# Zero writes to another queue, another order of experts and a rebuilt ending in a one-core transformer layer

## The chip, the cores and the metric

The program runs on 1 core of one Trainium2 chip. The metric is the device time of one execution in microseconds (us). The engines of the core are PE (TensorE; PEld is its weight load), DVE (VectorE), ACT (ScalarE), POOL (GpSimd) and SP (SyncE, which here only issues transfers). Transfers are issued by SP, ACT and POOL, each into a queue of its own, and are carried out by the core's 16 DMA engines.

## The reference, cut to what matters

One layer over 512 latent tokens of width 1024 and 256 context tokens: a modulated norm, one input projection, two branches (neighbourhood attention, and a gated DeltaNet that scans chunks of 64 tokens in two directions), an output projection, and then a mixture of 32 experts of which each token takes 4. The last part is

```
logits = xf @ w_router + b_router;  top_val, top_idx = top_k(logits, 4);  gates = softmax(top_val)
per expert:  g, u = split(x @ w1[e] + b1[e]);  h = min(g,7) * sigmoid(1.702*min(g,7)) * (clip(u,-7,7) + 1)
             y = h @ w2[e] + b2[e]
x = x1 + g2 * sum over the 4 experts of gate * y;   out = rmsnorm(x) * final_norm_w
```

w1 is (32, 1024, 2048), w2 (32, 1024, 1024), float32: 384 tiles of 1 MiB, all of which are read. Everything is computed to float32 accuracy; where a matmul uses the faster fp32r form, both operands are split into a high and a low part and three products are summed.

## The kernel before, in words

**Mixer** (`mixer`). Inputs and the first part of `w_mod` are loaded on SP (lines 923 to 949; `w_mod` in 16 loads of 512 KB through 4 buffers), the tokens are normalized, transposed and split, and then the input projection runs in pieces, whose weights ACT's queue loads (line 1005) and ACT and DVE split (lines 29, 30). `conv(2560, True)` makes the DeltaNet's v: six token tiles, each evicted by ACT (line 1391) and stored by ACT's queue to `vd` (line 1392). The planner that orders the instructions puts one on its engine as soon as its operands are there by the planner's own estimate; program order is its priority.

**Zeros.** `y4d` is a DRAM table of 2048 rows (token, choice), into which the experts scatter. It is cleared by nine stores from a small zero tile, eight of 1020 KB in pieces of 480 bytes and one small (lines 1338 to 1340). They stand before the DeltaNet's preparation in the program, on SP; they depend on nothing but the zero tile.

**Experts** (`moe`). Experts are ordered by load on the chip. A "large" one takes 128 token slots, a "small" one 64, and 16 are of each kind; expert 0 is large and fixed, then (before) odd ones are large and even ones small, and the last, 31, is small too. `Stream` loads the weight tiles in the order in which they are used, (e: gate half g), (e-1: w2), (e: up half u), four tiles each, through 10 buffers; `pump` issues the next load on SP when the tile ten places earlier is done. A small expert packs two half-width products into one bank, so that they run side by side. A large one runs g and u in plain float32 when e < 5, and in split fp32r from 5 on (`split_`); w2 is plain float32 always. From e = 2 on the order on PE, ACT and DVE is that of the program (`strict`). `fetch` gathers an expert's token rows from DRAM, `scatter` writes its weighted result to `y4d` (both on POOL's queue), except for experts 30 and 31, whose results are placed by one-hot matmuls (`last`).

**Second biases** (`second_bias`). At e = NE-2 = 30 the rows of b2 are loaded (SP), scaled by POOL, split by ACT and DVE; the gates are turned into a 96-row matrix by DVE and four transposes on PE.

**Ending** (lines 744 to 808). After the last expert's transposes the eight `y4d` tiles are taken, added on POOL and DVE to `x1` (lines 745 to 751); then comes a branch on the number of overflow blocks (`overflow`, line 596), and only after it the PE products into the output banks (`second`, `last`, `rest`), the last w2, the squares on ACT, and per token tile a reciprocal root on DVE in single-column instructions, two scalings by DVE (line 775) and the store (line 776). The weight tiles of the last w2 stand behind the `y4d` tiles in the stream:

```
self.order[-4:-4] = [(t, "y", c) for t in range(4) for c in range(2)]
```

Of the kernel before, what the change touches and what calls it, by code (L numbers as in the profile page):

```python
# [38 lines left out]
class Stream:  # L39
# [52 lines left out]

def small(e):

    return e == 31 or e > 0 and e % 2 == 0


def column(e):

    return e if e in (0, 31) else 15 + e // 2 if e % 2 == 0 else (e + 1) // 2  # L100
# [38 lines left out]
def moe(tc, ctx, cst, release, rps, rt, rtp, h2, hx, h2d, x1d, y4d, modd, w1, b1, w2, b2, fn_d, out, NE=32):  # L139
# [30 lines left out]
    PE, ACT, DVE = Engine(nc.tensor), Engine(nc.scalar), Engine(nc.vector)  # L170
# [61 lines left out]
    def split_(e):  # L232

        return not small(e) and e >= 5
# [78 lines left out]
    for i in range(4):  # L313
        nc.sync.dma_start(br[32 * i:32 * i + 32], dap(b1, 512 * (i // 2), [[2048, 32], [1024, 2], [1, 512]]))
# [94 lines left out]
    def second_bias(get, bs, Gt):  # L409

        br = get([96, 1024], F32, 0)
# [3 lines left out]
        nc.scalar.activation(bs, br, AF.Copy)  # L415
        nc.vector.tensor_tensor(bs[32:64], br[32:64], bs[32:64].bitcast(F32), op=OP.subtract)
        tmp = get([128, 16, 32], F32, 1)
        nc.vector.tensor_tensor(tmp, E, gt[:, :, None].to_broadcast([128, 16, 32]), op=OP.mult)
        G = get([128, 4, 3, 32], F32, 1)
        for i in range(3):  # L420
            nc.vector.tensor_reduce(G[:, :, i, :], tmp.rearrange("p (t k) e -> p t e k", k=4), axis=AX.X, op=OP.add)
        p = bank("tr")
        for t in range(4):
            nc.tensor.transpose(p[0:96, 128 * t:128 * t + 128], G[:, t].rearrange("p a e -> p (a e)"), ident)
        nc.scalar.activation(Gt, p[0:96, :], AF.Copy)
        nc.vector.tensor_tensor(Gt[64:96], p[64:96, :], Gt[64:96].bitcast(F32), op=OP.subtract)
# [82 lines left out]
    def mm(x, e, kind, after=None):  # L509
# [4 lines left out]
        p = [bank(tag) for _ in range(1 if s else 2)]  # L514
# [79 lines left out]
    def overflow(n, ovi, rowd, gatd):  # L594

        with tc.If(n > 0):
            with tc.For_i(0, n) as j:
                e = nc.values_load(ovi[0:1, bass.ds(j, 1)], min_val=0, max_val=31)
                with ExitStack() as s2:
                    lp = s2.enter_context(tc.tile_pool(name="ov_l", bufs=1))  # L600
                    pp_ = s2.enter_context(tc.tile_pool(name="ov_p", bufs=1, space=PSUM))
# [15 lines left out]
                    def tr(src, name):  # L617
                        T = lp.tile([128, 8, 128], F32, name=name)
                        for q in range(2):
                            p = pp_.tile([128, 4, 128], F32, name="tr", bufs=2)  # L620
                            for k in range(4):
                                nc.tensor.transpose(p[:, k, :], src[:, (4 * q + k) * 128:(4 * q + k + 1) * 128], ident)
                            nc.vector.tensor_copy(T[:, 4 * q:4 * q + 4], p)
                        return T

                    def lin(T, w, c0, b=None):
                        ps_ = [pp_.tile([128, 512], F32, name="mm%d" % i, bufs=2) for i in range(2)]
# [34 lines left out]
                    for t in range(4):  # L662
                        nc.vector.tensor_scalar(ot[:, t], iot, tf[:, t:t + 1], None, op0=OP.is_equal)
                        for i in range(2):
                            p = pp_.tile([128, 512], F32, name="mm%d" % i, bufs=2)
# [6 lines left out]
    def second(t):  # L672
        for n in range(2):
            LP[t, n] = bank(("h", "h", "tr", "y")[t])
            PE.matmul(LP[t, n], Gt[:, 128 * t:128 * t + 128], bs[:, 512 * n:512 * n + 512], start=True, stop=False)

    def last(t, i):

        for n in range(2):
            h = slice(64 * n, 64 * n + 64)  # L680
            PE.matmul(LP[t, n], ohT[i][h, t, :], yl[i][h, :], start=False, stop=i == 1)

    def rest(t):
        for n in range(2):
            PE.matmul(LP[t, n], ident, x1[:, t, 512 * n:512 * n + 512], start=False, stop=False)

    for e in range(NE + 1):
# [9 lines left out]
        if e == 4:  # L697
            wlo = hx.tile([128, 4, 1024], F32R, name="B")
        if e < NE:
# [6 lines left out]
            ahead(e, "u")  # L706
        if e == 2:
            strict[0] = False
            ovt = overflow_table()
            strict[0] = True  # L710
        if e == 3:
            strict[0] = False
            ovt = ovt()
            strict[0] = True
        if e == NE - 2:

            x1 = hx.tile([128, 4, 1024], F32, name="A")
            nc.sync.dma_start(x1, x1d.rearrange("(t p) d -> p t d", p=128))
# [4 lines left out]
            second_bias(areas([xp.tile([128, 1024], F32, name="yy", bufs=2) for _ in range(2)]), bs, Gt)  # L723
            for i in range(2):
                for t in range(1, 4):
                    nc.vector.tensor_scalar(tlast[:, i, t:t + 1], tlast[:, i, 0:1], -128.0 * t, None, op0=OP.add)
                for t in range(4):
                    nc.vector.tensor_scalar(ohT[i][:, t, :], iot, tlast[:, i, t:t + 1], None, op0=OP.is_equal)
        if e == NE:
            break  # L730
        if e:
            p = mm(TA.pop(e - 1), e - 1, "w2")
            if e < NE - 1:
                scatter(e - 1, weighted(e - 1, p, xp.tile([128, 1024], F32, name="yy", bufs=2)))
            else:
                weighted(e - 1, p, yl[0])
        nxt = e + 2 if 1 <= e < NE - 2 else None
# [7 lines left out]
    strict[0] = False  # L745
    for t in range(4):
        r = [stream.take(t, "y", c) for c in range(2)]
        nc.gpsimd.tensor_tensor(r[1][:, 0], r[1][:, 0], r[1][:, 1], op=OP.add)
        for q in (r[0][:, 0], r[0][:, 1], r[1][:, 0]):
            nc.vector.tensor_tensor(x1[:, t], x1[:, t], q, op=OP.add)  # L750
        stream.pump()
    xctx.close()
    pctx.close()
    overflow(*ovt)
    ps = pctx.enter_context(tc.tile_pool(name="moe_q", bufs=2, space=PSUM))

# [5 lines left out]
    strict[0] = True  # L762

    def squares(t):
        for n in range(2):
            ACT.activation(junk[:, 512 * n:512 * n + 512], LP[t, n], AF.Square, accum_out=sq[:, n, t:t + 1])

    def final(t):
        v = slice(t, t + 1)
        DVE.tensor_tensor(ss[:, 0, v], sq[:, 0, v], sq[:, 1, v], op=OP.add)  # L770
        DVE.tensor_scalar(ss[:, 1, v], ss[:, 0, v], 1.0 / 1024, 1e-6, op0=OP.mult, op1=OP.add)
        rsqrt1(nc, ss[:, 2, v], ss[:, 1, v], ss[:, 0, v])
        for n in range(2):
            c = slice(512 * n, 512 * n + 512)
            nc.vector.scalar_tensor_tensor(xf[:, t, c], LP[t, n], ss[:, 2, v], fnb[:, c], op0=OP.mult, op1=OP.mult)  # L775
        nc.sync.dma_start(out.rearrange("o (t p) d -> (o t) p d", p=128)[t], xf[:, t])

    for t in range(3):
        second(t)
        last(t, 0)  # L780

    def early(c):
        if c == 2:
            for t in range(3):
                rest(t)

    p = mm(TA.pop(NE - 1), NE - 1, "w2", early)
    weighted(NE - 1, p, yl[1])
    for t in range(3):
        last(t, 1)  # L790
        squares(t)
    second(3)
    rest(3)
    for i in range(2):
        last(3, i)
    squares(3)
    for t in range(4):
        final(t)
    pctx.close()
    wctx.close()  # L800
# [61 lines left out]
def rsqrt1(nc, r, v, t):  # L862

    nc.vector.tensor_scalar(r.bitcast(I32), v.bitcast(I32), -0.5, float(0x5F3759DF), op0=OP.mult, op1=OP.add)  # L864
    for c in (-3.0, -12.0, -768.0):
        nc.vector.scalar_tensor_tensor(t, r, v, r, op0=OP.mult, op1=OP.mult)  # L866
        nc.vector.scalar_tensor_tensor(r, t, c, r, op0=OP.add, op1=OP.mult)  # L867


def mixer(tc, ctx0, ctx, ctx2, cst, I, rope_d, mask_d, modd, x1d, h2d, y4d, rt, dbg=None, upto=99):  # L870
# [466 lines left out]

    for i in range(8):
        nc.sync.dma_start(dap(y4d, i * 2040, [[16384, 128], [120, 17], [1, 120]]), cst["zero"][:, None, :].to_broadcast([128, 17, 120]))
    nc.sync.dma_start(dap(y4d, 16320, [[16384, 128], [1, 64]]), cst["zero"][:, 0:64])  # L1340
# [582 lines left out]
```

## Time and profile before

| | us |
|---|---|
| runs, median of 3 (lowest to highest) | 1887.46 (1884.3 to 1888.91) |
| the profiled execution, its own time | 1889.57 |
| its span in the profile | 1887.5 |

Busy shares of the span on the page: PE 90%, DVE 50%, ACT 31%, POOL 14%; the DMA queues of SP, ACT and POOL hold 72.2%, 10.4% and 2.2% of the 16 engines' span. A busy PE is not a PE at its peak. Where the rows below are stretches, the columns are named with the first group.

### The profile page before, as it was taken

How to read it: one execution, taken by the hardware profiler on the slowest of the kernel's cores; microseconds unless marked ns; L12 is line 12 of the kernel's file. 1: busy time of each engine (PE TensorE's matmuls, PEld its weight loads, DVE VectorE, ACT ScalarE, POOL GpSimd, SP SyncE). 2: the span in 40 equal slices, each digit the busy share in tenths (PEclk: the TensorE clock that was granted, in tenths of full speed). 3: DMA queues.
4: the chain of work that ended last, by engine and by line, in shares of the span. 5: the costliest groups of instructions: out<-in, count | busy, mean ns of one | idle time of the engine just before them, and what ended most of it. 6: DMA issues, size and time to landing. Idle time of an engine off the chain costs nothing. (4 is left out here: it accounts for less than half of the span.)

```text
span 1887.5 us, 25145 instructions
## 1 busy us (share of the span) xinstructions
PE 1702.2 (90%) x9411; PEld 1031.8 (55%) x9411; DVE 952.7 (50%) x1555; ACT 590.6 (31%) x829; POOL 261.7 (14%) x251
## 2 busy tenths in 40 slices
PE   1798799999989988899999999999999999999666
PEld 0275587787767767444455545455545555455312
DVE  1246697883557676711254345444533553354243
ACT  1334347333235542100043224322422342243001
POOL 0030300323200241300010011011101110100020
PEclk7898999999999999899999999999999999999887
DMA  9845838756587653989999999999999999999991
GB/s 283 280 128 174 247 108 236 203 134 163 148 213 195 198 157 134 389 302 378 388 405 409 409 409 409 408 407 406 401 400 402 407 399 398 408 405 399 359 404 77
DMA packets 281122, 574.67 MB, mean 304 GB/s; under 512 B 79150, under 2 KB 142082, under 8 KB 280868
## 3 DMA queue, kind: packets, MB, share of 16 engines
q1 hardware_dynamic: 204248, 499.65, 72.2%
q10 hardware_dynamic: 69885, 57.00, 10.4%
q0 software_dynamic: 6864, 16.38, 2.2%
q8 instruction: 75, 1.23, 0.3%
q14 instruction: 50, 0.41, 0.1%
HBM read 529.68 MB, written 51.02 MB: 308 GB/s over the span
## 5 line engine op out<-in xcount | busy, mean ns | idle before, releaser
L165 PE MATMUL y<-raw,at 128*128 128x512 f32 (+1 forms) x1024 | 336.9, 595 | 0.0
L165 DVE TENSOR_TENSOR B<-raw,whi 128x2048 fp32r<-128x2048 f32 x104 | 236.6, 2289 | 162.3 <-ACT whi L165 162.2
L165 ACT ACTIVATE whi<-raw 128x2048 fp32r<-128x2048 f32 x104 | 198.6, 1915 | 119.1 <-DMA raw<-in_w_dram 92.0
L165 PEld LDWEIGHTS y<-raw,at 128*128 128x128 f32 (+1 forms) x1024 | 132.8, 164 | 186.0 <-issue 185.3
L165 PE MATMUL h<-raw,xts 128*64 128x512 f32 x1024 | 233.3, 598 | 0.0
L165 DVE TENSOR_SCALAR h<-h 128x512 f32<-128x512 f32 x96 | 65.0, 695 | 221.9 <-PE h L165 221.9
L1022 PE MATMUL pj<-hh,whi 128*128 128x512 f32 (+3 forms) x432 | 164.7, 384 | 6.8 <-ACT zb L1207 2.8
L1023 PE MATMUL pj<-hl,whi 128*128 128x512 f32 (+3 forms) x432 | 161.3, 376 | 0.0
L581 POOL DMA_INDIRECT y4d<-yy,rows x30 | 48.4, 1613 | 805.0 <-DVE yy L165 805.0
L1025 PE MATMUL pj<-hh,wlo 128*128 128x512 f32 (+3 forms) x432 | 159.1, 377 | 0.0
L165 PEld LDWEIGHTS h<-raw,xts 128*64 128x64 f32 x1024 | 68.1, 136 | 133.4 <-issue 132.8
L29 ACT ACTIVATE whi<-raw 128x512 fp32r<-128x512 f32 (+1 forms) x105 | 65.0, 626 | 188.9 <-PE pj L1023 78.2
L165 PE MATMUL h<-whi,xth 128*128 128x512 f32 x416 | 118.1, 406 | 6.4 <-ACT whi L165 6.2
L165 PE MATMUL h<-B,xth 128*128 128x512 f32 x416 | 116.1, 401 | 7.2 <-DVE B L165 7.2
L30 DVE TENSOR_TENSOR wlo<-raw,whi 128x512 fp32r<-128x512 f32 (+1 forms) x105 | 81.5, 781 | 70.1 <-ACT whi L29 68.5
L165 DVE SCALAR_TENSOR_TENSOR yy<-y,gates,g2b 128x512 f32<-128x512 f32 x32 | 24.0, 750 | 180.9 <-PE y L165 179.1
L165 PE MATMUL h<-whi,xtl 128*128 128x512 f32 x416 | 113.8, 395 | 0.0
L165 ACT ACTIVATE at<-tr 128x512 f32<-128x512 f32 x48 | 27.0, 596 | 258.2 <-PE tr L165 241.9
L1022 PEld LDWEIGHTS pj<-hh,whi 128*128 128x128 f32 (+1 forms) x432 | 82.4, 191 | 30.8 <-issue 4.6
L165 PEld LDWEIGHTS h<-B,xth 128*128 128x128 f32 x416 | 75.8, 188 | 35.9 <-DVE B L165 19.8
L165 PEld LDWEIGHTS h<-whi,xth 128*128 128x128 f32 x416 | 74.7, 188 | 34.1 <-ACT whi L165 17.7
L1023 PEld LDWEIGHTS pj<-hl,whi 128*128 128x128 f32 (+1 forms) x432 | 82.5, 191 | 14.8 <-issue 1.5
(485 smaller groups left out, 2460.1 us busy)
## 6 DMA issues: line engine op xcount, KB each, us to landing
raw<-in_w_dram SPq DMA_DIRECT2D x384, 1024.0 KB
raw<-in_w_in_dram ACTq DMA_DIRECT2D x44, 512.0 KB
raw<-in_w_mod_dram ACTq DMA_DIRECT2D x32, 512.0 KB
raw<-in_w_mod_dram SPq DMA_DIRECT2D x16, 512.0 KB
raw<-y4d SPq DMA_DIRECT2D x8, 1024.0 KB
y4d<-zero SPq DMA_DIRECT2D x8, 1020.0 KB
kk<-nkd SPq DMA_DIRECT2D x16, 384.0 KB
gad<-st ACTq DMA_DIRECT2D x16, 256.0 KB
```

The source lines that it names most:

```text
L29: nc.scalar.activation(hi, src, AF.Copy)
L30: nc.vector.tensor_tensor(lo, src, hi.bitcast(F32), op=OP.subtract)
L165: i = f(*a, **k)
L581: s = nc.gpsimd.indirect_dma_start(out=dst, out_offset=bass.IndirectOffsetOnAxis(ap=rows[:, k:k + 1], axis=0), in_=y, in_offset=None, boun ...
L1022: nc.tensor.matmul(p, h, mh(k), start=k == 0, stop=False)
L1023: nc.tensor.matmul(p, h, ml(k), start=False, stop=False)
L1025: nc.tensor.matmul(p, l, mh(k), start=False, stop=k == kb - 1)
```

## The change

It has these parts:

- **Zeros**: the nine stores go from SP to ACT's queue, two behind each store of v in four of the six token tiles (`issue_behind` fixes only the order of issue on that queue).
- **Order of experts**: 1 and 2 are small, then 15 large and 12 small ones are spread evenly over 3 to 29, 30 and 31 are small. Large ones are split from e = 3 on. The overflow table is made at e = 1 and closed at e = 2 (before 2 and 3).
- **First biases** b1 (four loads of 128 KB) go from SP's queue to POOL's.
- **Second biases**: b2 and `x1` are loaded by ACT's queue; the gate part runs behind expert 29's scatter, the transposed part behind expert 30's w2, all in program order.
- **Ending**: the `y4d` tiles of token tiles 0, 1 are loaded ahead of the last u, those of 2, 3 ahead of the last w2, and added there (`rows_of`); seven of the eight output banks get `second` and `last(., 0)` ahead of the last w2 and `rest` inside it; the reciprocal roots of token tiles 1 to 3 are taken together; two half tiles are scaled by ACT and POOL instead of DVE; the branch for overflow blocks comes behind the stores, and writes the output again if it is taken.

```
-        self.order[-4:-4] = [(t, "y", c) for t in range(4) for c in range(2)]
+        for i, t in ((-4, 2), (-12, 0)):
+            self.order[i:i] = [(t + c // 2, "y", c % 2) for c in range(4)]
+SMALL = [False, True, True] + [(12 * i + 25) // 27 > (12 * i + 13) // 27 for i in range(27)] + [True, True]
-        return not small(e) and e >= 5
+        return not small(e) and e >= 3
-        nc.sync.dma_start(br[32 * i:32 * i + 32], dap(b1, ...))
+        nc.gpsimd.dma_start(br[32 * i:32 * i + 32], dap(b1, ...))
-            nc.sync.dma_start(br[32 * i:32 * i + 32, :], b2.rearrange("o e f -> (o e) f"))
+            nc.scalar.dma_start(br[32 * i:32 * i + 32, :], b2.rearrange("o e f -> (o e) f"))
...
+    def rows_of(t):
+        r = [stream.take(t, "y", c) for c in range(2)]
+        POOL.tensor_tensor(r[1][:, 0], r[1][:, 0], r[1][:, 1], op=OP.add)
+        for q in (r[0][:, 0], r[0][:, 1], r[1][:, 0]):
+            DVE.tensor_tensor(x1[:, t], x1[:, t], q, op=OP.add)
+        stream.pump()
...
             else:
                 weighted(e - 1, p, yl[0])
+                turned_()
+                for t in range(2):
+                    rows_of(t)
...
     transp(NE - 1)
+    for t in range(2, 4):
+        rows_of(t)
+    p = [bank("y")]
+    seven = [(t, n) for t in range(4) for n in range(2)][:7]
+    for q in seven:
+        second(*q)
+        last(*q, 0)
+    def early(c):
+        if c == 2:
+            for q in seven:
+                rest(*q)
+    p = mm(TA.pop(NE - 1), NE - 1, "w2", early, p)
+    weighted(NE - 1, p, yl[1])
-    overflow(*ovt)
...
+    for q in seven:
+        last(*q, 1)
+    second(3, 1)
+    last(3, 1, 0)
+    rest(3, 1)
+    last(3, 1, 1)
+    for t in range(4):
+        squares(t, [LP[t, n] for n in range(2)])
+    factor(slice(0, 1))
+    for n in range(2):
+        scaled(0, n, LP[0, n])
+    store(0)
+    factor(slice(1, 4))
+    for t in (1, 2):
+        scaled(t, 1, LP[t, 1], True)
+    for t in (1, 2, 3):
+        scaled(t, 0, LP[t, 0])
+    for t in (1, 2):
+        store(t)
+    scaled(3, 1, LP[3, 1])
+    store(3)
...  copies of the eight banks to x1
+    overflow(*ovt)
+    with tc.If(ovt[0] > 0):
...
-    for i in range(8):
-        nc.sync.dma_start(dap(y4d, i * 2040, [[16384, 128], [120, 17], [1, 120]]), cst["zero"]...)
-    nc.sync.dma_start(dap(y4d, 16320, [[16384, 128], [1, 64]]), cst["zero"][:, 0:64])
...
-        nc.scalar.dma_start(vd[128 * t:128 * t + 128], v)
+        d = nc.scalar.dma_start(vd[128 * t:128 * t + 128], v)
+        for i in range(2 * t, min(2 * t + 2, 9)):
+            z = nc.scalar.dma_start(dap(y4d, i * 2040, ...), zeros)
+            issue_behind(tc, z.ins, d.ins)
```

## Rows read from the trace of the kernel before

**Rows 1.** Busy time by stretch, start: engines, PE clock, DMA share, GB/s
```profile
core 0: us, PE busy (x) PEld busy (x) DVE busy (x) ACT busy (x) POOL busy (x), PEclk, DMA share, GB/s
20.00:50.00 30.00, 3.29 (x16) 1.00 (x15) 1.85 (x3) 0.00 (x0) 0.00 (x0) 0.62 1.07 264
```
**Rows 2.** Timeline, start: us, us, instruction, count, [idle before, releaser]
```profile
13.73 30.03 SPq L1339 DMA_DIRECT2D y4d<-zero  x8
...
52.60 6.58 PE L949 MATMUL dn<-raw,sc 128*32 128x512 f32 x20 [29.31 <-DMA raw<-in_w_mod_dram]
```
**Rows 3.** Instructions of tile y4d: ns min/median/max, first and last start
```profile
L1339 SPq DMA_DIRECT2D y4d<-zero x8: 615/3787/6163, 13.7 to 39.6; - x8
```
**Rows 4.** Timeline of ACT: four issues, and the instruction behind them
```profile
383.00 2.48 ACTq L1302 DMA_DIRECT2D nvd<-st  x4
385.52 0.60 ACT L1297 ACTIVATE st<-pj 128x512 f32<-128x512 f32 x1 [2.56 <-DMA nvd<-st]
```
**Rows 5.** Instructions of tile vd: the stores of v
```profile
L1392 ACTq DMA_DIRECT2D vd<-v x6: 326/336/367, 307.1 to 325.2; - x6
```
**Rows 6.** Busy time by stretch, around and behind the stores of v
```profile
310.00:330.00 20.00, 18.72 (x154) 14.80 (x153) 7.80 (x18) 14.40 (x31) 0.00 (x0) 0.93 1.06 286
330.00:350.00 20.00, 18.20 (x300) 14.07 (x299) 14.40 (x36) 8.52 (x18) 4.26 (x6) 0.81 0.81 225
```
**Rows 7.** Busy time by stretch, experts: the first ones, and later
```profile
800.00:950.00 150.00, 149.03 (x482) 65.10 (x481) 28.95 (x52) 16.51 (x26) 10.16 (x10) 0.97 0.97 357
1000.00:1100.00 100.00, 100.00 (x421) 55.78 (x421) 51.91 (x42) 38.15 (x32) 9.79 (x8) 1.00 1.03 409
```
**Rows 8.** Timeline of PE: tiles of large and small experts
```profile
825.44 13.90 PE L165 MATMUL y<-raw,at 128*128 128x512 f32 x32
...
842.62 7.03 PE L165 MATMUL h<-raw,xth 128*128 128x512 f32 x16
...
895.95 7.09 PE L165 MATMUL y<-raw,at 128*64 128x512 f32 x32
...
948.69 1.10 PE L165 MATMUL h<-whi,xth 128*128 128x512 f32 x4
...
951.49 1.10 PE L165 MATMUL h<-whi,xth 128*128 128x512 f32 x4
```
**Rows 9.** Timeline of PE: the gate matrix of the second biases
```profile
1775.24 1.06 PE L424 MATMUL tr<-ident,yy 128*96 128x128 f32 x4 [15.24 <-DVE yy L421]
```
**Rows 10.** Busy time by stretch, the last experts and the end of the stream
```profile
1780.00:1795.00 15.00, 15.00 (x46) 6.06 (x46) 1.50 (x2) 0.00 (x0) 1.01 (x1) 1.00 0.92 323
...
1845.00:1850.00 5.00, 4.92 (x10) 2.02 (x12) 0.00 (x0) 0.00 (x0) 0.00 (x0) 0.50 0.10 41
```
**Rows 11.** Timeline, ending
```profile
1828.61 16.27 DVE L750 TENSOR_TENSOR A<-A,raw 128x1024 f32<-128x1024 f32 x8
...
1845.08 1.19 PE L165 MATMUL h<-B 96*128 96x512 f32 x2 [20.96 <-DVEq L596]
...
1859.13 3.70 PE L165 MATMUL h<-A,ident 128*128 128x512 f32 x8
...
1864.48 1.94 PE L165 MATMUL y<-raw,at 128*64 128x512 f32 x8
...
1866.53 0.75 DVE L165 SCALAR_TENSOR_TENSOR yl<-y,gates,g2s 128x512 f32<-128x512 f32 x1 [21.65 <-PE y L165]
...
1867.34 1.99 PE L165 MATMUL h<-yl,oh 64*128 64x512 f32 x8 [0.92 <-DVE yl L165]
...
1869.13 0.59 ACT L165 ACTIVATE junk<-h 128x512 f32<-128x512 f32 x1
...
1869.84 0.16 DVE L165 TENSOR_TENSOR ssf<-sqf 128x1 f32<-128x1 f32 x1 [2.56 <-ACT junk L165]
...
1872.07 1.41 DVE L775 SCALAR_TENSOR_TENSOR xf<-h,ssf,fnb 128x512 f32<-128x512 f32 x2 [0.35 <-DVE ssf L867]
...
1873.61 9.92 SPq L776 DMA_DIRECT2D out_dram<-xf  x4
```
**Rows 12.** Timeline of POOL: one product over 128x512
```profile
751.70 1.60 POOL L1846 TENSOR_TENSOR h<-h,s2b 128x512 f32<-128x512 f32 x1 [37.22 <-DVE mx L122]
```

More of the change, by code (lines that the diff above doesn't have):

```diff
@@ L90, in take @@
         return self.raw.pop(key)
+SMALL = [False, True, True] + [(12 * i + 25) // 27 > (12 * i + 13) // 27 for i in range(27)] + [True, True]
 def small(e):
-    return e == 31 or e > 0 and e % 2 == 0
+    return SMALL[e]
 def column(e):
-    return e if e in (0, 31) else 15 + e // 2 if e % 2 == 0 else (e + 1) // 2
+    return 16 * SMALL[e] + sum(x == SMALL[e] for x in SMALL[:e])
 class Route:
@@ L168, in __getattr__ @@
             return call
-    PE, ACT, DVE = Engine(nc.tensor), Engine(nc.scalar), Engine(nc.vector)
+    PE, ACT, DVE, POOL = (Engine(e) for e in (nc.tensor, nc.scalar, nc.vector, nc.gpsimd))
     nc.vector.tensor_copy(cnt, rtp[:, 128:160])
@@ L407, in places, with second_bias, gates_, turned_ @@
         return finish
-    def second_bias(get, bs, Gt):
-        br = get([96, 1024], F32, 0)
+    def second_bias(br, tmp, bs, Gt):
         for i in range(3):
-            nc.sync.dma_start(br[32 * i:32 * i + 32, :], b2.rearrange("o e f -> (o e) f"))
+            nc.scalar.dma_start(br[32 * i:32 * i + 32, :], b2.rearrange("o e f -> (o e) f"))
         nc.gpsimd.tensor_tensor(br, br, g2b[0:96], op=OP.mult)
[L415 to L426, printed above, removed]
+        G = tmp[:, 512:896].rearrange("p (t a e) -> p t a e", t=4, a=3)
+        tmp = tmp[:, 0:512].rearrange("p (i e) -> p i e", e=32)
+        def gates_():
+            DVE.tensor_tensor(tmp, E, gt[:, :, None].to_broadcast([128, 16, 32]), op=OP.mult)
+            for i in range(3):
+                DVE.tensor_reduce(G[:, :, i, :], tmp.rearrange("p (t k) e -> p t e k", k=4), axis=AX.X, op=OP.add)
+        def turned_():
+            ACT.activation(bs, br, AF.Copy)
+            DVE.tensor_tensor(bs[32:64], br[32:64], bs[32:64].bitcast(F32), op=OP.subtract)
+            p = bank("tr")
+            for t in range(4):
+                PE.transpose(p[0:96, 128 * t:128 * t + 128], G[:, t].rearrange("p a e -> p (a e)"), ident)
+            ACT.activation(Gt, p[0:96, :], AF.Copy)
+            DVE.tensor_tensor(Gt[64:96], p[64:96, :], Gt[64:96].bitcast(F32), op=OP.subtract)
+        return gates_, turned_
     def overflow_table():
@@ L513, in mm @@
         s = small(e)
-        p = [bank(tag) for _ in range(1 if s else 2)]
+        p = p or [bank(tag) for _ in range(1 if s else 2)]
         o = [p[0][0:64], p[0][64:128]] if s else p
@@ L619, in tr @@
                         for q in range(2):
-                            p = pp_.tile([128, 4, 128], F32, name="tr", bufs=2)
+                            p = bank("tr").rearrange("p (k s) -> p k s", k=4)
                             for k in range(4):
@@ L626, in lin @@
                     def lin(T, w, c0, b=None):
-                        ps_ = [pp_.tile([128, 512], F32, name="mm%d" % i, bufs=2) for i in range(2)]
+                        ps_ = [bank("h") for _ in range(2)]
                         if b is not None:
@@ L664, in overflow @@
                         for i in range(2):
-                            p = pp_.tile([128, 512], F32, name="mm%d" % i, bufs=2)
+                            p = bank("y")
                             v = slice(512 * i, 512 * i + 512)
@@ L670, in moe, with second, last, rest @@
     LP = {}
[L672 to L685, printed above, removed]
+    def second(t, n):
+        LP[t, n] = bank(("h", "h", "tr", "y")[t])
+        PE.matmul(LP[t, n], Gt[:, 128 * t:128 * t + 128], bs[:, 512 * n:512 * n + 512], start=True, stop=False)
+    def last(t, n, i):
+        h = slice(64 * n, 64 * n + 64)
+        PE.matmul(LP[t, n], ohT[i][h, t, :], yl[i][h, :], start=False, stop=i == 1)
+    def rest(t, n):
+        PE.matmul(LP[t, n], ident, x1[:, t, 512 * n:512 * n + 512], start=False, stop=False)
+    def rows_of(t):
[4 more added lines that the diff above has]
+        stream.pump()
     for e in range(NE + 1):
@@ L706, in moe @@
             ahead(e, "u")
+        if e == 1:
+            ovt = overflow_table()
         if e == 2:
[L708 to L711, printed above, removed]
             strict[0] = False
@@ L714, in moe @@
             strict[0] = True
+            wlo = hx.tile([128, 4, 1024], F32R, name="B")
         if e == NE - 2:
             x1 = hx.tile([128, 4, 1024], F32, name="A")
-            nc.sync.dma_start(x1, x1d.rearrange("(t p) d -> p t d", p=128))
+            nc.scalar.dma_start(x1, x1d.rearrange("(t p) d -> p t d", p=128))
             hb = hx.tile([128, 4, 1024], F32R, name="B")
@@ L722, in moe @@
             yl = [wk3.tile([128, 512], F32, name="yl", bufs=2) for _ in range(2)]
-            second_bias(areas([xp.tile([128, 1024], F32, name="yy", bufs=2) for _ in range(2)]), bs, Gt)
+            gates_, turned_ = second_bias(xp.tile([128, 1024], F32, name="xth", bufs=2)[0:96],
+                                          xp.tile([128, 1024], F32, name="xtl", bufs=2), bs, Gt)
             for i in range(2):
                 for t in range(1, 4):
-                    nc.vector.tensor_scalar(tlast[:, i, t:t + 1], tlast[:, i, 0:1], -128.0 * t, None, op0=OP.add)
+                    DVE.tensor_scalar(tlast[:, i, t:t + 1], tlast[:, i, 0:1], -128.0 * t, None, op0=OP.add)
                 for t in range(4):
-                    nc.vector.tensor_scalar(ohT[i][:, t, :], iot, tlast[:, i, t:t + 1], None, op0=OP.is_equal)
+                    DVE.tensor_scalar(ohT[i][:, t, :], iot, tlast[:, i, t:t + 1], None, op0=OP.is_equal)
         if e == NE:
@@ L744, in moe @@
     transp(NE - 1)
[L745 to L751, printed above, removed]
+    for t in range(2, 4):
[11 more added lines that the diff above has]
+    weighted(NE - 1, p, yl[1])
     xctx.close()
-    pctx.close()
-    overflow(*ovt)
-    ps = pctx.enter_context(tc.tile_pool(name="moe_q", bufs=2, space=PSUM))
+    wctx.close()
     tailp = inner.enter_context(tc.tile_pool(name="moe_t", bufs=1))
@@ L761, in moe, with squares, factor @@
     ss = sb.tile([128, 3, 4], F32, name="ssf")
-    strict[0] = True
-    def squares(t):
+    def squares(t, src):
         for n in range(2):
-            ACT.activation(junk[:, 512 * n:512 * n + 512], LP[t, n], AF.Square, accum_out=sq[:, n, t:t + 1])
-    def final(t):
-        v = slice(t, t + 1)
+            ACT.activation(junk[:, 512 * n:512 * n + 512], src[n], AF.Square, accum_out=sq[:, n, t:t + 1])
+    def factor(v):
         DVE.tensor_tensor(ss[:, 0, v], sq[:, 0, v], sq[:, 1, v], op=OP.add)
@@ L771, in final @@
         DVE.tensor_scalar(ss[:, 1, v], ss[:, 0, v], 1.0 / 1024, 1e-6, op0=OP.mult, op1=OP.add)
[L772 to L775, printed above, removed]
-        nc.sync.dma_start(out.rearrange("o (t p) d -> (o t) p d", p=128)[t], xf[:, t])
[L778 to L796, printed above, removed]
-    for t in range(4):
-        final(t)
+        rsqrtn(ss[:, 2, v], ss[:, 1, v], ss[:, 0, v], DVE)
+    def scaled(t, n, src, pool=False):
+        c = slice(512 * n, 512 * n + 512)
+        if pool:
+            ACT.activation(xf[:, t, c], src, AF.Copy, scale=ss[:, 2, t:t + 1])
+            POOL.tensor_tensor(xf[:, t, c], xf[:, t, c], fnb[:, c], op=OP.mult)
+        else:
+            DVE.scalar_tensor_tensor(xf[:, t, c], src, ss[:, 2, t:t + 1], fnb[:, c], op0=OP.mult, op1=OP.mult)
@@ new lines, in store @@
+    def store(t):
+        nc.sync.dma_start(out.rearrange("o (t p) d -> (o t) p d", p=128)[t], xf[:, t])
+    for q in seven:
[4 more added lines that the diff above has]
+    last(3, 1, 1)
+    for t in range(4):
+        squares(t, [LP[t, n] for n in range(2)])
[8 more added lines that the diff above has]
+        scaled(t, 0, LP[t, 0])
@@ new lines, in moe @@
+    for t in (1, 2):
+        store(t)
+    scaled(3, 1, LP[3, 1])
+    store(3)
+    for (t, n), p in LP.items():
+        if n:
+            ACT.activation(x1[:, t, 512 * n:512 * n + 512], p, AF.Copy)
+        else:
+            DVE.tensor_copy(x1[:, t, 512 * n:512 * n + 512], p)
+    strict[0] = False
+    overflow(*ovt)
+    with tc.If(ovt[0] > 0):
+        for t in range(4):
+            squares(t, [x1[:, t, 512 * n:512 * n + 512] for n in range(2)])
+        factor(slice(0, 4))
+        for t in range(4):
+            for n in range(2):
+                scaled(t, n, x1[:, t, 512 * n:512 * n + 512])
+            store(t)
@@ L799, in moe @@
     pctx.close()
-    wctx.close()
     inner.close()
@@ L859, in rsqrt, with rsqrtn @@
             nc.vector.scalar_tensor_tensor(r, t, 1.5, r, op0=OP.add, op1=OP.mult)
-def rsqrt1(nc, r, v, t):
-    nc.vector.tensor_scalar(r.bitcast(I32), v.bitcast(I32), -0.5, float(0x5F3759DF), op0=OP.mult, op1=OP.add)
+def rsqrtn(r, v, t, e):
+    e.tensor_scalar(r.bitcast(I32), v.bitcast(I32), -0.5, float(0x5F3759DF), op0=OP.mult, op1=OP.add)
     for c in (-3.0, -12.0, -768.0):
-        nc.vector.scalar_tensor_tensor(t, r, v, r, op0=OP.mult, op1=OP.mult)
-        nc.vector.scalar_tensor_tensor(r, t, c, r, op0=OP.add, op1=OP.mult)
+        if r.shape[1] == 1:
+            e.scalar_tensor_tensor(t, r, v, r, op0=OP.mult, op1=OP.mult)
+        else:
+            e.tensor_tensor(t, r, r, op=OP.mult)
+            e.tensor_tensor(t, t, v, op=OP.mult)
+        e.scalar_tensor_tensor(r, t, c, r, op0=OP.add, op1=OP.mult)
 def mixer(tc, ctx0, ctx, ctx2, cst, I, rope_d, mask_d, modd, x1d, h2d, y4d, rt, dbg=None, upto=99):
@@ L1391, in mixer @@
         nc.scalar.activation(v, p, AF.Silu)
-        nc.scalar.dma_start(vd[128 * t:128 * t + 128], v)
+        d = nc.scalar.dma_start(vd[128 * t:128 * t + 128], v)
+        for i in range(2 * t, min(2 * t + 2, 9)):
+            z = cst["zero"][:, None, :].to_broadcast([128, 17, 120]) if i < 8 else cst["zero"][:, 0:64]
+            z = nc.scalar.dma_start(dap(y4d, i * 2040, [[16384, 128], [120, 17], [1, 120]] if i < 8 else [[16384, 128], [1, 64]]), z)
+            issue_behind(tc, z.ins, d.ins)
         dump("V", v, lambda d, t=t: d[:, t, :])
```

10 lines of the change are left out of this document (4 added, 6 removed).

## The prediction

> **What bounds the kernel now.** I read the page's slices first, then busy time by stretch, and went into the timeline wherever the DMA rate or PE fell. Three places matter.
>
> At the start PE, DVE, ACT and POOL are all but idle from 20 to 50 us while the DMA engines are full [rows 1]. The timeline says with what: the planner has put the eight large zero stores into SP's queue at 13.7 us, ahead of twelve of the sixteen `w_mod` loads; they hold SP for 30 us, and PE waits 29.3 us for `w_mod` [rows 2]. Nothing else can run: every normalized token needs that modulation.
>
> In the experts' part the reader should look at GB/s. From 1000 us on it is 409, DMA share 1.03: the weight stream is the bound, and PE, though shown busy, only follows it. From 800 to 950 us it is 357 with PE busy 149 of 150 us: there PE is the bound and the stream waits for buffers [rows 7].
>
> At the end the stream is dry at about 1845.5 us (41 GB/s over 5 us is half a microsecond of transfer) [rows 10]. PE has idled 21 us by then, because its next products stand behind the branch, and that behind eight DVE additions that take 16.3 us [rows 11]. So 1887.5 - 1845.5 = 42 us pass between the last weight and the end.
>
> **The change part by part.** The sum is made against the profiled execution (1889.6 us, span 1887.5), 2.1 us above the median of the runs.
>
> *Zeros leave SP's head: -29.5.* PE's wait of 29.3 us goes, and the ninth, small store with it. What is late next is `w_mod` itself, which then follows at the pace that it had behind the zeros, so I count the wait whole.
>
> *Zeros on ACT's queue: +20 (0 to +55).* The stores of v are issued from 307 to 325 us [rows 5]; the small zero store and four pairs of large ones come behind five of them. One large store takes its issuer 0.6 us if the queue is empty, 3.79 us when the one before it is still being drained, and 6.16 at the longest, when other loads were ahead of it [rows 3]. An engine that issues is held: behind four issues of 2.48 us in all ACT's next instruction had waited 2.56 us [rows 4]. What is queued behind on ACT are the evictions of v and the high parts of the projection weights, for which DVE and PE wait; the loads of those weights stand in the same queue. PE is busy 18.7 of 20 us here, so it has little to give, and the DMA engines are full (1.06), then at 0.81 [rows 6]. Lower bound: each pair's hold falls into ACT's 5.6 idle us and the stalls are made up later, near 0; less than nothing is excluded, since work is only added there. Upper bound: the other transfers take every second turn, 8 x 2 x 3.79 = 61, less 5.6 = 55. I take 0.6 + 5.7 a pair (the second near the long hold, since other loads are ahead here too): 25, less ACT's idle 5.6, about 20.
>
> The Trainium skill bears on this (page "DMA: Bandwidth & Descriptors", section "Issuing engines are not separate DMA queues"): transfers run on the same 16 engines whichever engine issues them and interleave, and another issuer saves only time to issue. By that rule the 30.3 us of transfer (8 x 3.79) are moved and not removed, and where the DMA engines are full they are paid in full; it is the second rival below.
>
> *Order of experts, split from 3 on: -15 (-5 to -19).* The stretch from 800 to 950 us falls short of 409 GB/s by 52 x 150 / 409 = 19 us [rows 7]. Per tile PE needs 3.5 us in plain float32 (7.03 for two, 13.90 for four), 1.8 for a small expert (7.09 for four) and 2.8 when split [rows 8], against 2.56 us of transfer (1.05 MB at 409 GB/s). Before, experts 0, 1 and 3 are plain and large, so PE loses 0.9 us a tile and the ten buffers are full at 800. After, 1 and 2 are small: PE needs about 22 us an expert against 31 of transfer, and 3 is split. What stays is w2 of expert 0, four tiles of 3.5 us, 3.8 us late. Later two large ones stand side by side at times; a split large expert costs PE about 6 us more than its transfer, which the ten buffers (25 us) take, and the small ones give back 8. The upper end is the whole shortfall, the lower one that these pairs stop the stream now and then. The table's DVE work one expert earlier hides behind PE, which runs 22 us and more an expert; uncovered it would be a few us. b1 on POOL's queue: 0, since SP waits at that point for the experts' order anyway; if POOL were late there, four issues at the 0.6 us of [rows 4] would cost 2.5.
>
> *Second biases: -3 (-6 to 0).* PE waits 15.2 us for the gate matrix [rows 9], and the stream then sinks to 323 GB/s over 15 us, which is (409 - 323) x 15 / 409 = 3.2 us [rows 10]. Only those count, not the 15 us, as the stream is the bound. The same bytes are still loaded; issuing them holds ACT, which is nearly idle.
>
> *Ending: -15 (-18 to -8).* From the landing T of the last tile: the third tile lands at T-2.6 and takes 1.9 us; seven `rest` of 0.93 (3.70 for four) 6.5; the last tile 1.9: T+7.7; weighting 0.75: T+8.5 [rows 11]. Then eight `last` at 0.5 and the eighth bank's other three products, 5.8: T+14.3, the squares (0.59 each) behind it by one: T+15.3. The joint root is 12 small DVE instructions where nine took 2.2 us with their waits: 2.5, T+17.8. Four halves on DVE at 0.7 end at T+20.6; ACT 0.6 and two POOL products of 1.6 [rows 12] at T+21.6. The last of four store issues began by about 1883.2 and the end came 4.3 us later, so T+26, and 1 us for two branches: T+27 against T+42. DVE's additions hide under the last u and w2 tiles, since those of tiles 2 and 3 need 6 us each and their rows land 10 us ahead of T. Uncovered they would cost up to 6, which with a slow branch makes the lower end.
>
> Sum: -29.5 + 20 - 15 - 3 - 15 = -42.5, so 1847 in a profiled execution, and 1845 as a median.
>
> **The rivals.**
>
> *Zeros nearly free.* ACT has 11.5 idle us in the 20 us behind, and PE's later waits for the scan could swallow the rest: +3 instead of +20, 1828. Against it: ACT's idle time there is often a wait for PE, and both stall together.
>
> *Moved, not hidden.* With the DMA engines at 1.06 the zeros interleave with stores that the scan waits for, and each pair holds ACT for twice the drain of one store and more: +40 in place of +20, 1865. The rule quoted above is the argument for it, and rows 6 agree as far as 330 us; the 0.81 behind it speaks against.
>
> *PE stays the bound at the first experts.* If the stretch from 800 us is slow for the gathers and scatters in it, or two large experts in a row stop the stream, the 15 us don't come: 1860. For it: DMA share is 0.97 there, not far below 1. Against: PE's 3.5 us a tile explains the rate.
>
> *Slower.* Turns could be dealt by packet, 480 bytes of zeros against packets of 2 KB and more: three times 3.79 us a store, 91 us, less 5.6 of idle ACT = 85. Then 1845 + 65 = 1910. It decides from the point where the hold eats 62.5 us of other gains, 8.5 us a store; 6.16 is the longest seen.
>
> **How the numbers follow.** Forecast 42%, zeros nearly free 18%, moved 18%, first experts unchanged 13%, slower 6%; 3% for an order by the planner that loses more elsewhere, within no change. The range 1822 to 1872 takes in the first four but for their tails, about 80%. The likeliest case's own range is 1836 to 1854. A change of 0.3% is about what a measurement of this kernel can tell from none: faster 0.91, same 0.03, slower 0.06.
>
> **What would show it.** After, `w_mod` should be through PE 29 us earlier; behind each store of v ACT should be held by two zero stores, 20 to 30 us in all, with PE idle near there. GB/s should stand near 405 from 800 us on. The last weights should land near 1818, PE should start the last products at once, and the end come 27 us later. I am wrong on the zeros if the first weight tile of the experts is issued 20 us earlier or more, or not earlier at all; on the experts if the rate from 30 us behind their start is still below 380; on the ending if more than 32 us lie behind the last weight.

## The result and the profile after

The changed kernel takes 1873.13 us (median of 13 runs, 1863.86 to 1881.82) against 1887.66 (13 runs): ratio 0.9922 [0.9902, 0.9942]. It is faster, by 14.5 us, where I forecast 42.5; 1873 lies just outside my range. The profiled execution took 1870.34 us, span 1868.5, so the two spans differ by 19.0 us, and the account is made between these two. They are single executions, and the medians are only 14.5 us apart; a second trace of the changed kernel, after_again, has a span of 1870.7 us and its first expert weight at 751.5:

| stretch of the span | before | after | gained | forecast |
|---|---|---|---|---|
| start to the first expert weight on SP | 745.5 | 749.0 | -3.5 | 9.5 |
| from there to the dry stream | 1100 | 1086.5 | 13.5 | 18 |
| dry stream to the end | 42 | 33 | 9 | 15 |

The start does what was forecast. First busy time by stretch, then SP's timeline (start us, us, instruction, count), both after; they answer to [rows 1, 2].

```profile
20.00:50.00 30.00, 22.43 (x92) 5.42 (x91) 4.25 (x11) 4.34 (x8) 0.00 (x0) 0.89 0.68 212
```
```profile
7.14 30.24 SPq L993 DMA_DIRECT2D raw<-in_w_mod_dram  x16
...
44.26 0.69 DVE L996 COPY mrow<-dn 128x512 f32<-128x512 f32 x1 [21.75 <-PE dn L994]
```

The 16 loads of `w_mod` follow each other, PE is busy 22.4 of 30 us instead of 3.3, and the first modulation row is copied at 44.26 us (70.63 before): 26.4 us won. At the stores of v all of it goes. The stretch behind them, ACT's timeline in it, and PE's wait there:

```profile
300.00:350.00 50.00, 23.71 (x326) 18.35 (x325) 12.76 (x27) 13.99 (x30) 1.85 (x2) 0.73 0.94 237
```
```profile
304.70 0.45 ACTq L1433 DMA_DIRECT2D vd<-v  x1
305.18 6.06 ACTq L1437 DMA_DIRECT2D y4d<-zero  x2
311.34 3.93 ACTq L1433 DMA_DIRECT2D vd<-v  x1
315.31 5.30 ACTq L1437 DMA_DIRECT2D y4d<-zero  x2
320.66 1.15 ACT L29 ACTIVATE whi<-raw 128x512 fp32r<-128x512 f32 x2 [17.65 <-DMA vd<-v]
```
```profile
PE pj L1067 <- ACT whi L29: 16.2, 1, 16.2
PE dn L1500 <- ACT X L1493: 8.8, 1, 8.8
```

PE works 23.7 of 50 us here; before it was busy over 18 of 20 [rows 6]. ACT stands behind zeros, a store of v, zeros; PE waits 16.2 us for the high part of a weight that ACT would have made. The last store of v begins at 335.2 us, 10 later than before [rows 5], although the first came 24.5 us earlier; by the first expert weight the start has lost 29.9 us. The row of those weights, after, has 745.5 as its first start before:

```profile
L83 SPq DMA_DIRECT2D raw<-in_w_dram x384: 12/2148/6013, 749.0 to 1820.2; - x192
```

The experts, after, against [rows 7]; then a stretch behind them, and the second biases and the dry stream against [rows 10]:

```profile
800.00:950.00 150.00, 143.43 (x591) 69.49 (x592) 58.47 (x68) 39.84 (x40) 13.33 (x11) 0.98 1.02 396
...
1200.00:1225.00 25.00, 25.00 (x89) 10.12 (x87) 3.46 (x5) 2.11 (x4) 1.20 (x2) 1.00 1.00 374
...
1780.00:1795.00 15.00, 12.06 (x53) 3.41 (x51) 2.16 (x4) 2.13 (x3) 0.00 (x0) 1.00 1.03 409
...
1835.00:1840.00 5.00, 5.00 (x21) 1.68 (x18) 0.00 (x0) 0.00 (x0) 0.00 (x0) 1.00 0.10 38
```

The ending, after, against [rows 11]:

```profile
1822.97 0.48 PE L170 MATMUL h<-B 96*128 96x512 f32 x1
1823.39 1.12 PE L170 MATMUL h<-yl,oh 64*128 64x512 f32 x2
...
1833.32 5.37 PE L170 MATMUL y<-raw,at 128*64 128x512 f32 x24
...
1838.62 3.70 PE L170 MATMUL h<-A,ident 128*128 128x512 f32 x8
...
1844.83 1.94 PE L170 MATMUL y<-raw,at 128*64 128x512 f32 x8
...
1847.62 1.99 PE L170 MATMUL h<-yl,oh 64*128 64x512 f32 x8 [0.85 <-DVE yl L170]
...
1853.54 8.29 SPq L802 DMA_DIRECT2D out_dram<-xf  x4
...
1853.79 1.12 PE L170 MATMUL y<-yl,oh 64*128 64x512 f32 x2
...
1862.53 0.68 DVE L170 COPY A<-y 128x512 f32<-128x512 f32 x1
```

PE has hardly a pause from 1822.6 to 1846.7 us. Read by the same rule as before, the stream is dry at T = 1835.5.

### The profile page after: what moved, and what is told of

Read it like the earlier page. It is cut to its first block, busy times and chain, and to the rows that moved or that the text cites. A ratio compares the mean times of both kernels' runs of the same rounds, so it can differ in the third digit from the quotient of the medians.

```text
span 1868.5 us, 25316 instructions
## 1 busy us (share of the span) xinstructions
PE 1701.3 (91%) x9475; PEld 1047.0 (56%) x9475; DVE 986.8 (53%) x1562; ACT 623.6 (33%) x851; POOL 272.9 (15%) x257
## 5 line engine op out<-in xcount | busy, mean ns | idle before, releaser
L170 DVE TENSOR_TENSOR B<-raw,whi 128x2048 fp32r<-128x2048 f32 x120 | 273.5, 2290 | 170.6 <-ACT whi L170 170.3
L170 PE MATMUL y<-raw,at 128*64 128x512 f32 (+1 forms) x1024 | 336.7, 594 | 3.7 <-DMA raw<-in_w_dram 3.7
L170 ACT ACTIVATE whi<-raw 128x2048 fp32r<-128x2048 f32 x120 | 229.3, 1915 | 151.0 <-DMA raw<-in_w_dram 111.3
L170 PE MATMUL h<-raw,xts 128*64 128x512 f32 x1024 | 238.6, 608 | 13.7 <-DMA raw<-in_w_dram 13.6
L170 PEld LDWEIGHTS y<-raw,at 128*64 128x64 f32 (+1 forms) x1024 | 132.3, 163 | 190.3 <-issue 182.6
L170 PE MATMUL h<-whi,xth 128*128 128x512 f32 x480 | 137.1, 407 | 10.3 <-ACT whi L170 10.1
L170 PE MATMUL h<-B,xth 128*128 128x512 f32 x480 | 133.3, 399 | 6.1 <-DVE B L170 5.8
L170 PE MATMUL h<-whi,xtl 128*128 128x512 f32 x480 | 131.3, 395 | 0.0
L170 PEld LDWEIGHTS h<-whi,xth 128*128 128x128 f32 x480 | 86.3, 188 | 41.7 <-ACT whi L170 24.8
L170 PEld LDWEIGHTS h<-B,xth 128*128 128x128 f32 x480 | 87.9, 188 | 37.1 <-DVE B L170 18.0
L170 PEld LDWEIGHTS h<-whi,xtl 128*128 128x128 f32 x480 | 90.1, 188 | 21.7
```

What stands on the lines that cost most here:

```text
L170: i = f(*a, **k)
```

## The experiments

The question was first where the 26 us of the start go. Theory A: an issuer is held. Theory B: the DMA engines are full there. Theory C: a later stage takes back whatever is won. The planner orders each engine's work anew for each kernel; where an order is the same as its mate's, it is said.

**z_pool_v: another issuer, same place.** 1881.7 us, ratio 0.9959 [0.9939, 0.9979].

```
-            z = nc.scalar.dma_start(dap(y4d, ...), z)
+            z = nc.gpsimd.dma_start(dap(y4d, ...), z)      # waits for the eviction of v
```

> The zeros stay where they are in time, two stores behind the eviction of each tile of v, but GpSimd's queue issues them instead of ScalarE's. Theory A (ScalarE is held by its full queue, and DVE and PE wait for ScalarE; that is where the 26 us won at the start go): ScalarE runs free from 285 to 345 us, PE is busy over 40 of 50 us from 300 to 350 (23.7 now), and the kernel takes 1873 - 25 = 1848 us. Theory B (the DMA engines are full there, at a share of 0.99 to 1.15, so 30 us of transfer are paid whoever issues them): 1868 to 1875 us, the last store of v near 335 us as now.

POOL issues each zero store in 0.8 to 1.3 us and nothing of it stands on ACT's queue. SP's timeline, ACT's, the issues of the stores of v (ns min/median/max), and PE's wait:

```profile
293.55 13.53 SPq L1420 DMA_DIRECT2D ad<-AT  x4
307.12 11.29 SPq L1457 DMA_DIRECT2D R<-ad  x2
```
```profile
309.21 11.03 ACTq L1433 DMA_DIRECT2D vd<-v  x2
...
320.29 0.63 ACT L29 ACTIVATE whi<-raw 128x512 fp32r<-128x512 f32 x1 [20.59 <-DMA ad<-AT]
```
```profile
L1433 ACTq DMA_DIRECT2D vd<-v x6: 326/326/346, 283.8 to 333.3; - x6
```
```profile
PE pj L1067 <- ACT whi L29: 16.0, 1, 16.0
```

Theory A falls: the zeros are off ACT's queue, each of its own stores of v is issued in 0.33 us, and PE's wait is the same 16 us. Now the transfers of others are held: four stores of 64 KB take SP 13.5 us to issue (2.67 for four at 279 us of the same run), and the 11.0 us of ACT's row are two short issues with a wait between them, by the profile for one of these 64 KB stores (`ad<-AT`) to land. Theory B has the mechanism right but not the time: 1881.7 us lies above its 1868 to 1875. The Trainium skill (page "DMA: Bandwidth & Descriptors", section "Issuing engines are not separate DMA queues") says that transfers of all issuers share the same 16 engines; this run agrees.

**z_small: twice the packets.** Every engine has the same instructions in the same order. 1912.5 us, ratio 1.0131 [1.0085, 1.0177].

```
-            z = cst["zero"][:, None, :].to_broadcast([128, 17, 120])        # 480 bytes a piece
+            z = cst["zero"][:, None, 0:60].to_broadcast([128, 34, 60])      # 240
```

> Same order of every instruction as the changed kernel and the same bytes; only the zero stores behind v are cut into packets of 240 bytes instead of 480, so twice as many. If the price of the zeros there is packets (a store of 480-byte packets moved 275 GB/s while the weight stream moves 409), the transfers take up to 30 us longer and the other stores and loads of the stretch wait for them: 1890 to 1905 us, last store of v near 350 us or later. If it is bytes, or only the count of issues: 1870 to 1876.

39 us for the same bytes, more than I expected. Two stretches of it (the changed kernel moved 277 GB/s from 300 to 325 us), and its stores of v:

```profile
300.00:325.00 25.00, 11.04 (x92) 8.41 (x90) 0.90 (x2) 4.53 (x11) 0.00 (x0) 0.64 1.33 152
325.00:350.00 25.00, 4.17 (x10) 2.96 (x10) 1.29 (x2) 1.63 (x3) 0.00 (x0) 0.53 1.27 134
```
```profile
L1433 ACTq DMA_DIRECT2D vd<-v x6: 327/342/9422, 280.7 to 365.4; - x6
```

The DMA engines stay full and move about half. So the price here is the engines' time, for pieces this small that time goes by their number and not by their bytes, and the path pays it. The Trainium skill (the same page, section "Why small descriptors are slow (HBM only)") gives 27% overhead for 256 bytes from a fixed cost of 3 cycles a packet; by that, as an estimate, half the size would cost 17% more. The run shows 277 / 152 = 1.8 times, and the measurement decides.

**z_pool_late and z_late_wide: a quiet place.** 1844.64 us, 0.9778 [0.9742, 0.9814], and 1844.68, 0.9774 [0.9758, 0.9790].

```
     nc.gpsimd.tensor_tensor(a2b, a2b, n2b, op=OP.mult)
+    # all nine stores on nc.gpsimd, ordered behind this instruction
```

> The nine zero stores go to GpSimd's queue behind its last work on the second norm's scale, near 716 us, where the DMA engines are used to 0.26 and GpSimd is idle for 37 us. Theories A and B both say that the loss from 285 to 345 us goes: first expert weight issued near 720 instead of 749, 1873 - 29 = 1844 us; if the 8 MB take longer than to 750 us, up to 10 us of it come back as a slower start of the weight stream (1854). Theory C (what is won at the start is lost again on any way to the experts, because a later stage is bound by its own loads): 1865 to 1873 us and the first weight near 745.

> As the run with the zeros near 716 us, but from a zero tile of 256 columns, 1024 bytes a packet instead of 480, in eight stores. If the small packets cost the DMA engines time (a store of 1.04 MB took 3.79 us, 275 GB/s, against the weight stream's 409), the stores are done 5 to 10 us earlier and the weight stream starts at full rate: 0 to 8 us less than that run. If a packet's size doesn't matter here, the same time within 2 us.

All 28.5 us come. With the start so much shorter, GpSimd's place was at 681 us and not at 716. The zeros and the first weight of z_pool_late, and its stretch in which the changed kernel issued the zeros:

```profile
L1863 POOL DMA_DIRECT2D y4d<-zero x9: 587/1288/1551, 681.5 to 692.1; - x9
```
```profile
L83 SPq DMA_DIRECT2D raw<-in_w_dram x384: 367/2146/5999, 715.4 to 1794.4; - x192
```
```profile
283.00:340.00 57.00, 52.90 (x634) 44.54 (x633) 41.27 (x95) 30.76 (x58) 10.70 (x14) 0.94 0.83 232
```

Weights begin 33.6 us earlier than in the changed kernel. Some 8 of these don't reach the end of the profiled span (1842.9): the stream takes 1095 us instead of 1086.5, its first 50 us at 354 GB/s with the last zeros among them. Theory C falls. In the medians the larger pieces change nothing. In the traces they are faster: from 684 to 710 us the engines move 341 GB/s instead of 280, and the profiled span is 3.3 us shorter (1839.6 against 1842.9), which is within the spread of these runs. The count of packets is not the difference: on GpSimd's queue 8.9 MB went in 2400 packets in one run and 2368 in the other, some 3.7 KB each, though the source has pieces of 480 bytes in one.

**z_sp_head: the zeros alone undone.** 1869.62 us, 0.9882 [0.9835, 0.9930]; first weight at 745.9.

```
-            z = nc.scalar.dma_start(dap(y4d, ...), z)      # behind the stores of v
+    nc.sync.dma_start(dap(y4d, ...), ...)                  # nine stores where they stood before
```

> Of the change the zeros alone are undone: nine stores from SP's queue, where the planner puts them ahead of most of w_mod, as before. By the traces the zeros behind the stores of v win 26 us at the start and lose 29.5 until the first expert weight. If that is the whole account (theory B, DMA engines full at v): first weight near 745.5 us, 1866 to 1873 us, no slower than the change. If the forecast's account held (-29.5 + 20), 1882 us.

Moving the zeros to ACT's queue is worth nothing that these runs can tell; what the change gains comes from its other parts.

**b4_late: the zeros alone, on the kernel before.** 1862.69 us, 0.9870 [0.9845, 0.9895]. The edit is that of z_late_wide on the kernel before.

> The kernel before with one edit: the zeros leave SP's head and go behind GpSimd's work near 716 us. If the 29.3 us that PE waited for w_mod carry through to the end whenever the zeros are hidden, 1887.5 - 29 = 1858 us, up to 4 more if the stream starts slower, first weight near 716. If something on the way to the experts takes them back whatever the place of the zeros, over 1875.

This one edit gains 26 us, more than the whole change; the first weight comes at 712.1 us, 33.4 earlier than before, and the stream gives some of it back. With z_sp_head it shows that the halves nearly add: 26 us from a quiet place and 20 from the rest, 43 when both are there (z_late_wide).

**exp_old: the order of the experts alone undone.** 1880.0 us, 0.9957 [0.9932, 0.9983], against 0.9922 [0.9902, 0.9942].

```
-    return SMALL[e]
+    return e == 31 or e > 0 and e % 2 == 0
...  the columns of the gates follow this order
-        return not small(e) and e >= 3
+        return not small(e) and e >= 5
```

> Of the change the order of the experts alone is undone: 1 large, 2 small, alternating, split products from expert 5 on. By the forecast's step 1873 + 15 = 1888 us (+5 to +19), with GB/s from 800 to 850 us back near 310. By the rival (the first experts' stretch is bound by the gathers or by two large experts in a row, so that the order wins nothing) 1873 +- 3 us.

7 us, between the two theories; the intervals overlap, so the stream is the better witness. It runs from 745.8 to 1840.8 us here, 1095 against 1086.5: the order is worth 8.5. From the first issue of a weight to the last it is 1079.5 us here, 1071.2 in the changed kernel and 1070.6 in that kernel's second trace.

```profile
800.00:950.00 150.00, 149.63 (x492) 66.14 (x491) 30.54 (x51) 18.30 (x27) 10.16 (x10) 0.99 0.99 371
...
1200.00:1600.00 400.00, 388.49 (x1557) 206.96 (x1556) 183.50 (x155) 127.84 (x111) 40.81 (x24) 1.00 1.02 402
```

From 800 to 950 us the order wins (396 - 371) x 150 / 409 = 9 us. Of the 14 us by which the changed kernel beats the kernel before in this stretch, 5 stay with this kernel, so by this trace another part of the change brings them (the overflow table stands one expert earlier in both). Behind 1200 us the changed kernel has single stretches of 374 GB/s, as the one shown above, where PE works without a pause: the w2 of a large expert takes it 13.90 us from 1206.47 on, as long as before the change [rows 8], in 10.2 us of transfer.

**The ending: end_if and wide_none.** end_if 1878.77 us, 0.9950 [0.9928, 0.9971]; wide_none 1838.78, 0.9720 [0.9672, 0.9768].

```
-    for (t, n), p in LP.items(): ...copies of the banks to x1
     strict[0] = False
+    with tc.If(ovt[0] > 0): ...the same copies                 # end_if
-    overflow(*ovt); with tc.If(ovt[0] > 0): ...                 # wide_none: copies and branch gone
```

> Only the ending differs from the changed kernel: the eight copies of the output banks to x1 stand inside the branch for further blocks, which isn't taken. Theory D (the end waits for the copies, 2.4 us of DVE behind the last scaled half, and for the branch behind them): 2 to 3 us less, 1870.5. Theory E (the last stores set the end, since their bytes move until 1865 us): the same within 0.5 us.

> The zeros near 716 us in packets of 1024 bytes (1844.7 us), and in addition the copies of the output banks and the branch for further blocks behind the stores are left out, so rows of experts with more than one block of tokens beyond their first are not computed. If the end waits for copies and branch, as the last store's issue at 1861.8 and the end at 1868.5 in the changed kernel suggest against 4.3 us before: 2.4 us less, 1842; if the stores' own bytes and their completion take the 6.7 us: the same within 0.5 us in the distance from the last store's issue to the end.

In end_if the planner put two of the four stores behind the new branch: its issues run from 1853.43 to 1864.25 us, its end is 1868.6, so the copies saved were spent on later stores, and the run says nothing on theory D. Why its median lies 5.6 us above the changed kernel's stays open. In wide_none the last store was issued by 1834.74 and the end is 1839.4, 4.7 us against 6.7 in the changed kernel (1861.83 to 1868.5) and 6.7 in z_late_wide, its mate: copies and branch cost 2 us behind the stores, about what theory D said. In the medians this is lost in the spread (1830.8 to 1845.7).

**end_early, with its mate wide_again.** Only PE's order differs. 1843.27 us, 0.9752 [0.9727, 0.9776], against 1846.74, 0.9774 [0.9741, 0.9808]: not told apart.

```
+        if e == NE - 1: second(0,0), last(0,0,0), (0,1), (1,0)      # ahead of the last u
-        if c == 2: rest(*q) for seven
+        if c in (0, 2): rest(*q) for four, then three
```

> The kernel with the zeros near 716 us in 1024-byte packets, and of its ending only the order on PE changed: the second biases and the products of the last expert but one of three of the seven banks (4.5 us) stand ahead of the last u products, where PE waits for weights, and four of the seven rests (3.5 us) behind the first tile of the last w2. Theory F (from the last u products on PE has no pause, so the ending is bound by PE's line of products and not by the last tile's landing): from the dry stream to the end 28 us instead of 32, 1844.7 - 4 = 1841 us. Theory G (the landing of the last tile and the tail of DVE, ACT and stores set it): within 1 us of the same kernel without the edit.

> The kernel with the zeros near 716 us in 1024-byte packets once more, as the mate of the run with the changed order on PE: 1844.7 us within 3.

The profiled span is 1.4 us shorter, not 4, and that comes from the start: the first weight is issued at 713.3 us against 718.6. From the end of the last u products (1790.0 and 1793.7 us) to the end of PE's last product (1826.6 and 1828.1) end_early takes 36.6 us, its mate 34.4. Ten microseconds of both with the same kind of work, end_early first (the last three numbers are PEclk, DMA share, GB/s):

```profile
1795.00:1805.00 10.00, 10.00 (x15) 2.81 (x16) 6.84 (x4) 0.00 (x0) 4.25 (x2) 0.50 0.66 265
```
```profile
1797.00:1807.00 10.00, 10.00 (x22) 3.08 (x22) 7.64 (x5) 0.14 (x1) 5.76 (x2) 1.00 0.71 286
```

PE has no pause in either, but in end_early it ran at 0.50 of its clock (1.2 GHz), 15 products instead of 22. In it PE had been busy 1.48 of the 3 us from 1790 on, the clock fell at 1793.5 and was back at 1.00 at 1807.1; its mate had been idle from 1773.9 to 1784.1, worked at 0.50 to 1789, and was back at 1.00 when this line began. Three pairs, 4.5 us of products, were taken out of PE's line (the four rests only changed their place in it), and half of the 13.6 us at 0.50, an estimate of 6.8, was added by the clock: that is the 2.2 us by which the line grew. So the ending is PE's line of products, as theory F has it. Whether the 4.5 us would come at full clock stays open.

**after_again.** 1873.36 us, 0.9917 [0.9887, 0.9947].

> The changed kernel once more on the chip of these runs: 1873 us within 5.

It repeats the first result.

## Why the prediction was wrong, step by step

**Zeros leave SP's head, -29.5: nearly right.** 26.4 by the modulation row, which is copied at 41.4 to 44.7 us in the twelve traces without zeros at SP's head, 26 to 29 earlier than before; the missing 3 are within that spread. That the median of b4_late also gains 26.4 is chance: its first weight comes 33.4 us earlier.

**Zeros on ACT's queue, +20: this step failed; it was +29.9.** I priced the hold of ACT and took its idle 5.6 us off. The runs show another mechanism: the stretch [rows 6] was at a DMA share of 1.06, and 30.3 us of transfer cost the path 29.9 (some 3 more in the second trace); with the other issuer it was no less. The first expert weight comes 3.5 us late, which was my mark for wrong. That is my own second rival, by its condition, though not at its price: I gave it 40, by doubling a held pair, where the plain transfer time was the answer. I argued against it from the share of 0.81 behind 330 us. That was the mistake: in the new time the zeros were issued from 283 to 340 us, and up to 325 the share was 0.99 and then 1.15. Those shares hold the zeros themselves; without them it is 0.83 from 283 to 340 us in z_pool_late and 0.87 in z_late_wide, which would leave room for 7 to 10 of the 30 us (0.13 or 0.17 x 57), and not even these were hidden. Why not is not shown; z_pool_v shows what the path waits for, small transfers that land late among the zeros.

**Order of experts, split from 3: -15, measured -8.5.** The mechanism is right (396 GB/s against 357, above the 380 I had set), and 14 us come in its stretch; the order itself brings 9 of them. What I mis-sized is its share: of the 19 us of shortfall 5 go without the order (exp_old), and another 5 stay (396 against 409). Little is given back behind the stretch, where the rate dips to 374, the "now and then" of my lower end: 402 GB/s from 1200 to 1600 us in exp_old, 400 in the changed kernel.

**Second biases, -3: right by the trace,** though no run has them alone. 323 GB/s became 409 in their stretch, which is the 3.2 us. With the old order of experts the stream is 5 us shorter than before, and these are among them.

**b1 on POOL, 0: nothing in the trace speaks against it;** it was not run alone.

**Ending, -15: -9, too large by 6.** Over 32 us lie behind T, my own mark for wrong. The term that failed is PE's line ahead of the last tile. I had its third tile done at T-0.7 and the rests next; but seven pairs of `second` and `last` (10.4 us, 1822.97 to 1833.32) stand first, the third tile ends at T+3.1, the last tile at T+11.3 instead of T+7.7, the last product at T+19.4 instead of T+14.3: 5.1 of the 6 us. I counted the work that came off PE's wait and not how much of it must now fit between the last u and T. And I priced a `last` at 0.5, which it costs only beside its mate: `last(t, 0, .)` and `last(t, 1, .)` use different halves of 128 rows, and where they stand next to each other PE takes them side by side, four of them in 1.82 us (1847.62 to 1849.44); alone between two `second` one takes 1.05 (1823.39 to 1824.44), both at a clock of 1.00. In the kernel before they stood two and two. By these prices the order second, last, second, last costs 3.6 us ahead of the tiles and the eighth bank's two lone `last` 1.1, an estimate of 4.7 of the 5.1 us; no run has them in pairs. The rest is behind the last store: copies and branch 2 us, where I had 1.

Sum: 9.9 at the zeros, 3.1 at `w_mod`, 4.5 in the stream, 6 at the end are the 23.5 by which the span of this one execution was missed.

## What to carry to other kernels

A transfer that is moved costs nothing only where the DMA engines have room for it: read the share in slices as short as the transfer, not over the stage. When they are full, ask for the transfer's time, and not for who issues it; and count its pieces. When an idle engine's work is pulled ahead of an event, add up the whole line that must now fit before that event, with each product at its price in its new place: one that ran beside its mate may cost twice as much alone.

## What the runs showed of the hardware

The same broadcast source of 480-byte pieces left ACT's queue in over 19,000 packets (11.23 MB with its neighbours, 283 to 345 us) and POOL's in 2163 packets for 8.28 MB. The time of the engines follows the pieces and not these packets: by the trace's packet records, added up over the 16 engines, the zeros took 34.4 us in 17,408 packets of 480 bytes and 30.8 us in 1,920 of 4,320. Yet on POOL's queue the zeros hurt the other queues more: the weights began at 755.5 us against 749.0. How the engines deal turns between queues with packets of different sizes would have to be tried by itself. The rest of that run's 8 us over the changed kernel stays open too: its stream moved 347 GB/s in its second 50 us, against 370, for which no row gives a reason.

PE's clock was seen at 0.50 in the middle of a line of products without a pause, from 1793.5 to 1807.1 us of end_early, behind a stretch with several short waits; that cost end_early more than its order had won.
